# Every third V row of block 3 and every second of the sample goes to TensorE in the layer 1 mixer of a two-layer encoder

## The chip, the cores and the metric

The kernel runs on one core of a Trainium2 chip, as one program. The metric is its device time in microseconds (us). TensorE (PE) multiplies matrices into PSUM, VectorE (DVE), ScalarE (ACT) and GpSimd (POOL) work on tiles in SBUF, SyncE (SP) only issues transfers, and 16 DMA engines carry all of these.

## What is computed

Two layers, each a mixer and then PEER, a mixture of 16384 one-row experts. There are 512 prompt tokens (four blocks b0 to b3 of 128) and 64 sample tokens (s). Of the reference this matters here:

```python
# peer_u, peer_v: (2, 16384, 1024) float32; 8 heads, 16 experts for each head and token
x = x + jnp.concatenate([o_da, o_ml, o_cm], axis=-1) @ w_out   # end of the mixer
xn2 = rmsnorm(x, norm2_g)
x = x + peer(xn2, peer_wq, peer_keys, peer_u, peer_v)
...
# peer, for a block xi: e (t, 8, 16) experts by top-k of q @ keys, g their softmax
act = gelu(einsum('thkd,td->thk', u_tab[e], xi))
return einsum('thk,thkd->td', (g * act), v_tab[e])             # sum over 128 rows of v_tab
```

So each token needs 128 rows of `peer_u`, and then the sum of 128 rows of `peer_v`, each times one number.

## The kernel before

**Two ways to do PEER.** Two blocks of a layer are dense (b0 and b1 in layer 0, b2 and b3 in layer 1): in `peer_dense` every expert is computed, 128 at a time (a chunk): 8 matmuls of `U` into `H` (L1059), gelu on ACT (L1068), the gate product on DVE (L1092), and 4 matmuls of `V` into `y` (L1099). The other tokens are gathered. For each of a block's 128 expert slots `gather` (L960) has POOL fetch one row for each of the 128 partitions, 512 KB in all, into one of six `row` buffers. `gather_u` multiplies it with `xn` on DVE and sums along the row (L984); `gather_v` does

`x = row * hb[:, k] + x`

on DVE (L996), where column k of `hb` holds the gate times the activation of slot k. The sample has 64 such slots, since its two halves of experts lie on two halves of the partitions; at its end L1001 and L1002 add the lower half to the upper through a transfer (`up`).

**The order.** The stages of a layer stand in `ORDER`: for layer 1 norm (N1), projections (P1, Q1), attention and recurrence (M1), output projection (O1), expert scores (S1) of b0, b1 and s, then the same for b2 and b3 (N2 to O2), with the choice of experts of the first group (F1) among them. A scheduler lays out each engine's instructions in advance, from priorities and modelled times; the engines then run these orders, waiting on semaphores. Gathered rows have a low priority (`low`) and fill gaps. b3's V rows of layer 0 are left for layer 1: stage R, woven into M1, calls `rest_v`, which emits four rows at a time, each tied behind the last DVE instruction emitted by then. In the trace they run from 1776 to about 2040 us, the sample's U rows of layer 1 from about 2080, its V rows from 2231 to 2355, and the rows of b0 and b1 from 2510 to 3546, beside the dense blocks.

**PSUM** has eight banks of 128x512 f32. In the mixer they are `mm` (4, projections, attention, recurrence), `tr` (3, transposes) and `o` (1), by `PS_BUFS`. `LAG` says how many chunks `H` runs ahead of `y` in `peer_dense`.

**Norms.** A norm's reciprocal root (`rstd`, L226 to L231) is a chain of eleven tiny DVE instructions. In attention it ends in L608 and L609 (`on`), which PE waits for to transpose (L214) and to project (L396). The norm before the scores scales by a diagonal that ACT makes (L204, `dr`), and PE multiplies with it (L216).

Of the kernel before, what the change touches and what calls it, by code (L numbers as in the profile page):

```python
# [9 lines left out]
F32 = mybir.dt.float32  # L10
# [5 lines left out]
AF = mybir.ActivationFunctionType  # L16
ALU = mybir.AluOpType
AX = mybir.AxisListType
PSUM = bass.MemoryType.PSUM
DRAM = bass.MemoryType.DRAM  # L20

P = 128
# [21 lines left out]
MID = 10 ** 6  # L44
LOW = 10 ** 7
PS_TAG = {"p": "mm", "a": "mm", "r": "mm", "o": "o", "tp": "tr", "ta": "tr", "tr": "tr"}
PS_BUFS = {"mm": 4, "tr": 3, "o": 1}
T_TAG = {"p": "t", "a": "t", "r": "tr"}
T_BUFS = {"t": 4, "tr": 2}
DENSE_T = 4  # L50
LAG = [4, 8]
PRE = [1, 2]
EARLY_LEADS = 5
REST_STEP, REST_PARTS = 4, 16
# [38 lines left out]
def weave(*streams):  # L93
    live = [[g, n, 0] for g, n in streams]
    while live:
        r = min(live, key=lambda r: r[2] / r[1])
        r[2] += 1
        try:
            next(r[0])
        except StopIteration:  # L100
            live.remove(r)


def run(gen):
    for _ in gen:
        pass
# [14 lines left out]
class Build:  # L121
# [16 lines left out]
    def mixer_pools(self, ec, l):  # L138
        tc = self.tc

        def pool(name, bufs, **k):
            return ec(tc.tile_pool(name=name, bufs=bufs, reuse_waits="tile", **k))
        self.kvp = pool("kv", 1)
        self.mx = pool("mix", 1)
        self.t2 = pool("tmp", 1)
        self.xg = pool("xg", 1)
        self.wp = pool("wts", 3)
        self.whp = None if l else self.gp
        self.pm = pool("pmm", 1, space=PSUM)
        self.mixer = True  # L150

    def dense_pools(self, ec, l):
        tc = self.tc
# [24 lines left out]

    def psum(self, shape, st="p"):
        tag = PS_TAG[st] if self.mixer else "mm"  # L180
        ps = self.pm.tile([P] + list(shape), F32, tag=tag, name="ps", bufs=PS_BUFS[tag] if self.mixer else 3)
        return ps

    def ptile(self, st="p"):
# [804 lines left out]
        if t.sample:  # L989
            nc.vector.memset(x[NS:P], 0.0)  # L990

    def gather_v(self, t, k0, k1, tie=None):
        nc, n, x = self.nc, t.n, self.x[t.name]
        for k in range(k0, min(k1, t.npair)):
            row = self.gather(t, "peer_v", k)
            op = nc.vector.scalar_tensor_tensor(x, row, t.hb[:, k:k + 1], x, op0=ALU.mult, op1=ALU.add)  # L996
            if tie is not None:
                self.behind(op, tie)
        if t.sample and k1 >= t.npair:
            up = self.ca.tile([P, DM], F32, tag="xn", name="up", bufs=1)  # L1000
            nc.sync.dma_start(up[:NS], x[NS:P])  # L1001
            nc.vector.tensor_tensor(x[:n], x[:n], up[:n], op=ALU.add)  # L1002
# [6 lines left out]

    def rest_v(self, t, step):  # L1010
        for k in range(0, t.npair, step):
            self.low(self.gather_v, t, k, min(k + step, t.npair), self.last_dve())
            yield

    def gate_batch(self, blocks, i0, t0, pb):
# [32 lines left out]
    def peer_dense(self, l, group, xT):  # L1048
        nc, h, lag = self.nc, self.h, LAG[l]
        ys = [self.py.tile([P, 2, 512], F32, tag=f"y{i}", name=f"y{i}") for i in range(len(group))]  # L1050
# [66 lines left out]
    def run(self):  # L1117
        tc = self.tc
        self.S = Tok("s", NS, None)
        self.B = [Tok(f"b{i}", P, i) for i in range(4)]  # L1120
        self.setup()
        S, B = self.S, self.B
        g1, g2 = [B[0], B[1], S], [B[2], B[3]]
        for t in [S] + B:
            t.npair = 64 if t.sample else P
            t.c0 = TD if t.sample else (t.blk % 2) * P
        for l in range(DEPTH):
            D = g2 if l else g1[:2]
            for i, t in enumerate([S] + B):
                t.dense, t.order, t.early = t in D, i, t.sample  # L1130
            self.sel = self.ca.tile([P, TD // 8, 4, 8], F16, tag="sel", name="sel")
            self.select_pool()
            with ExitStack() as es:
                self.mixer_pools(es.enter_context, l)
                L = self.layer_params(l)
                steps = {
                    "N1": lambda: [(self.norm_in(l, L, g1), 1)], "N2": lambda: [(self.norm_in(l, L, g2), 1)],
                    "P1": lambda: [(self.project_a(l, L, g1), 4)], "Q1": lambda: [(self.project_b(l, L, g1), 2)],
                    "P2": lambda: [(self.project_a(l, L, g2), 4)], "Q2": lambda: [(self.project_b(l, L, g2), 2)],
                    "M1": lambda: self.mix(l, L, g1), "M2": lambda: self.mix(l, L, g2),  # L1140
                    "O1": lambda: [(self.out_proj(l, g1), 2)], "O2": lambda: [(self.out_proj(l, g2), 2)],
                    "S1": lambda: [(self.scores(l, L, g1), 18)], "S2": lambda: [(self.scores(l, L, g2), 18)], "F1": lambda: [(self.finish_select(l, g1), 3)],
                    "R": lambda: [(self.rest_v(B[3], REST_STEP), REST_PARTS)]}
                for part in ORDER[l].split():
                    weave(*[s for k in part.split("+") for s in steps[k]()])
                if l == 0:
                    self.low(lambda: run(self.finish_select(l, g2)), by=MID)
            with ExitStack() as es:
                self.dense_pools(es.enter_context, l)
                nlead = LAG[l] + 8 * PRE[l]  # L1150
                if l == 0:
                    xT = self.split(self.dx.tile([P, KC, TD], F32, tag="xTd", name="xTd"))
                    self.norm_T(D, Q_G2, L, xT)
                    dense = self.peer_dense(l, D, xT)
                    weave((self.first_gate(l), 32), (itertools.islice(dense, nlead), nlead))
                else:
                    sc = self.scores(l, L, g2)
                    next(sc)
                    dense = self.peer_dense(l, D, self.xT2)
                    weave((itertools.islice(dense, EARLY_LEADS), EARLY_LEADS), (sc, 18))  # L1160
                    run(itertools.islice(dense, nlead - EARLY_LEADS))
                    run(self.finish_select(l, g2))
                    self.gated = self.last_dve()
                    self.close_scores(es.enter_context, l)
                    run(self.first_gate(l))
                run(dense)
            for t in [S] + B:
                if not t.dense:
                    self.low(self.gather_u, l, L, t, None if l and t.sample else self.gated)
                    if l or t is not B[3]:  # L1170
                        self.low(self.gather_v, t, 0, P)
        self.fg = self.lp.tile([P, R_N], F32, tag="row", name="fg")[:, :DM]
        self.nc.sync.dma_start(self.fg, self.bcast_rows(self.h["final_g"], DM))
        for t in [S] + B:
            self.final(t)
# [91 lines left out]
```

## Time and profile before

| | us |
|---|---|
| time, median of 3 runs | 3598.27 |
| lowest and highest run | 3591.49, 3602.72 |
| profiled run: time | 3593.99 |
| its span, first to last instruction | 3592.2 |
| PE, DVE, ACT busy in the span | 3078.9, 2568.6, 669.8 |
| layer 0 (mixer, dense) | 0 to 640, 640 to 1640 |
| layer 1 mixer | 1640 to 2510 |
| layer 1 choice of experts, gates; dense to the end | 2510 to 2680; 2680 to 3592 |

1.79 us of the profiled run lie around its span. Busy time of an engine is the time in which at least one of its instructions runs, so a share near 1 in a stage means that the engine has no gap there, not that it works at its peak. The granted clock is that of TensorE as a share of 2.4 GHz, as a mean over the stretch (its two levels are 1.2 and 2.4 GHz).

### The profile page before, as it was taken

The numbers are of one execution on the slowest core, as the hardware profiler recorded it, in microseconds if no ns is written. First come the engines' busy times: TensorE is split into PE (matmuls) and PEld (weight loads), VectorE is DVE, ScalarE is ACT, GpSimd is POOL, SyncE is SP. The second block draws the span as 40 slices with busy tenths as digits, with TensorE's granted clock in tenths as the row PEclk, the third lists the DMA queues.
The fourth block names the chain that finished last, engine by engine and source line by source line (L and its number), as shares of the span: only waits on it lengthen the run. The fifth ranks groups of instructions, "written<-read, shape, count | busy, mean of one in ns | idle before, by whom it ended". The sixth has DMA issues, their size and how long they took to land.

```text
span 3592.2 us, 41429 instructions
## 1 busy us (share of the span) xinstructions
PE 3078.9 (86%) x13384; PEld 2057.7 (57%) x13384; DVE 2568.6 (72%) x5915; ACT 669.8 (19%) x2589; POOL 1540.9 (43%) x1284
## 2 busy tenths in 40 slices
PE   8989877789999999996977896589636999999996
PEld 6767646646666666653543654267512666666663
DVE  4454777776787666667688898847997679666664
ACT  4444222400121000001221222122210012000000
POOL 0000000065545445547657335610777666565562
PEclk9999989889999999998978997699858999999998
DMA  5332322289999999999979687853989999999995
GB/s 182 101 98 82 95 91 86 80 327 409 386 341 392 409 407 398 409 409 376 352 225 349 237 317 276 287 192 114 339 290 380 409 386 358 404 397 393 407 400 214
DMA packets 299929, 1060.21 MB, mean 295 GB/s; under 512 B 36372, under 2 KB 39232, under 8 KB 299712
## 3 DMA queue, kind: packets, MB, share of 16 engines
q0 software_dynamic: 184320, 671.17, 49.7%
q1 hardware_dynamic: 115392, 386.38, 29.9%
q8 instruction: 107, 1.75, 0.2%
q14 instruction: 110, 0.90, 0.1%
HBM read 1048.09 MB, written 8.27 MB: 294 GB/s over the span
## 4 chain that ended last, share of the span: by engine, by line
PE 44%; DVE 17%; DMA 16%; issue 14%; POOL 7%; ACT 2%; SPq 0%; POOLq 0%; DVEq 0%; ACTq 0%
PE H L1059 12%; PE y L1099 11%; DMA row<-in_peer_v_dram,idx 10%; PE ps L396 7%; POOL row L960 7%; PE ps L407 6%; DVE row L984 4%; DMA row<-in_peer_u_dram,idx 3%; DVE x_b L996 2%; PE ps L216 1%; PE ps L1028 1%; PE ps L572 1%; PE ps L830 1%; PE ps L574 1%; DVE o L1020 1%
## 5 line engine op out<-in xcount | busy, mean ns | idle before, releaser
L960 POOL DMA_INDIRECT row<-in_peer_u_dram,idx x640 | 776.6, 1213 | 1456.4 <-DVE row L984 822.4
L960 POOL DMA_INDIRECT row<-in_peer_v_dram,idx x640 | 764.1, 1194 | 542.4 <-DVE x_b L996 277.6
L984 DVE SCALAR_TENSOR_TENSOR row<-row,xn 128x1024 f32<-128x1024 f32 x640 | 769.8, 1221 | 178.1 <-DMA row<-in_peer_u_dram,idx 169.0
L1099 PE MATMUL y<-V,A 128*128 128x512 f32 x1856 | 845.4, 604 | 32.2 <-DMA V<-in_peer_v_dram 32.0
L996 DVE SCALAR_TENSOR_TENSOR x_b<-row,hb,x_b 128x1024 f32<-128x1024 f32 x512 | 656.2, 1282 | 158.5 <-DMA row<-in_peer_v_dram,idx 150.0
L1099 PEld LDWEIGHTS y<-V,A 128*128 128x128 f32 x1856 | 356.2, 194 | 421.5 <-issue 398.5
L1059 PE MATMUL H<-xT,U 128*128 128x256 f32 x2048 | 475.3, 385 | 35.2 <-ACT A L1068 20.4
L1059 PE MATMUL H<-xTd,U 128*128 128x256 f32 x2048 | 468.5, 382 | 10.2 <-ACT A L1068 8.2
L1059 PEld LDWEIGHTS H<-xT,U 128*128 128x128 f32 x2048 | 384.5, 191 | 125.8 <-ACT A L1068 39.4
L1059 PEld LDWEIGHTS H<-xTd,U 128*128 128x128 f32 x2048 | 386.7, 191 | 103.9 <-issue 40.4
L407 PE MATMUL ps<-xT,w 128*128 128x320 f32 (+1 forms) x1280 | 336.4, 417 | 28.3 <-DMA w<-in_wt_dram 17.2
L1068 ACT ACTIVATE A<-H 128x256 f32<-128x256 f32 x232 | 88.9, 383 | 1346.2 <-PE H L1059 751.2
L407 PEld LDWEIGHTS ps<-xT,w 128*128 128x128 f32 x1280 | 244.3, 195 | 95.4 <-issue 13.3
L1092 DVE TENSOR_TENSOR A<-A,W 128x256 f32<-128x256 f32 x232 | 96.8, 422 | 217.5 <-ACT A L1068 209.6
L1030 ACT ACTIVATE W<-ps 128x64 f32<-128x64 f32 x1024 | 137.8, 321 | 295.7 <-PE ps L1028 202.7
L1028 PE MATMUL ps<-o,o 128*128 128x64 f16 x2048 | 85.9, 199 | 119.6 <-DVE o L1024 119.6
L996 DVE SCALAR_TENSOR_TENSOR x_s<-row,hb,x_s 128x1024 f32<-128x1024 f32 x128 | 164.1, 1282 | 32.9 <-DMA row<-in_peer_v_dram,idx 31.1
L1028 PEld LDWEIGHTS <-o 128*128 128x128 f16 x2048 | 79.9, 102 | 151.5 <-DVE o L1024 75.4
L1099 PE MATMUL y<-V,pre 128*128 128x512 f32 x192 | 105.0, 704 | 38.9 <-DMA V<-in_peer_v_dram 31.1
L396 PE MATMUL ps<-w,xT 128*128 128x512 f32 (+3 forms) x320 | 128.9, 554 | 5.7 <-DMA w<-in_wn_dram 5.7
L351 DVE TENSOR_TENSOR wl<-w,wh 128x1024 fp32r<-128x1024 f32 (+1 forms) x56 | 64.4, 1150 | 75.9 <-PE ps L396 56.0
L396 PE MATMUL ps<-w,mix 128*128 128x512 f32 (+1 forms) x224 | 110.9, 648 | 5.8 <-DMA w<-in_wn_dram 4.2
(314 smaller groups left out, 3004.6 us busy)
## 6 DMA issues: line engine op xcount, KB each, us to landing
V<-in_peer_v_dram SPq DMA_DIRECT2D x256, 512.0 KB
U<-in_uT_dram SPq DMA_DIRECT2D x256, 512.0 KB
w<-in_wt_dram SPq DMA_DIRECT2D x96, 512.0 KB
w<-in_wn_dram SPq DMA_DIRECT2D x80, 512.0 KB
row<-in_peer_u_dram,idx POOLq DMA_INDIRECT x640
row<-in_peer_v_dram,idx POOLq DMA_INDIRECT x640
w<-in_keysT_dram SPq DMA_DIRECT2D x16, 256.0 KB
w<-in_wn_dram SPq DMA_DIRECT2D x8, 264.0 KB
```

The source lines that it names most:

```text
L351: self.nc.vector.tensor_tensor(lo, src, hi.bitcast(F32), op=ALU.subtract)
L396: self.nc.tensor.matmul(p[:t.n, :wd], x[kk][:, t.c0:t.c0 + t.n], ww[:, k * wd:(k + 1) * wd], start=(kk + part + j == 0), stop=(kk == KC - ...
L407: self.nc.tensor.matmul(ps, ww[:, k * P:(k + 1) * P], x[k][:, :n], start=(k + part + j == 0), stop=(k == KC - 1 and part == pair and j == ...
L960: self.nc.gpsimd.indirect_dma_start(out=row, out_offset=None, in_=self.h[tab], in_offset=bass.IndirectOffsetOnAxis(ap=t.idx[:, k:k + 1], a ...
L984: nc.vector.scalar_tensor_tensor(row, row, 1.0, xn, op0=ALU.mult, op1=ALU.mult, accum_out=hb[:, k:k + 1])
L996: op = nc.vector.scalar_tensor_tensor(x, row, t.hb[:, k:k + 1], x, op0=ALU.mult, op1=ALU.add)
L1028: nc.tensor.matmul(pb[:, j, :nq], o2[:, j // 2, :, j % 2], o1[:, p, j // 2, :, j % 2], start=(p == 0), stop=(p == 1))
L1030: nc.scalar.activation(W[:, :, t0:t0 + 8].rearrange("p i t -> p t i"), pb[:, :, 8 * i:8 * i + 8], AF.Copy, scale=1.0 / GSCALE)
L1059: mm = nc.tensor.matmul(hp, U[:, k, :], xT[k], start=(k == 0), stop=(k == KC - 1))
L1068: nc.scalar.activation(a, hp, AF.Gelu)
L1092: gated = nc.vector.tensor_tensor(a, a, Ws[ci // 8][:, ci % 8, :], op=ALU.mult)
L1099: nc.tensor.matmul(ys[i][:, hf, :], a[:, i * P:(i + 1) * P], V[:, hf * 512:(hf + 1) * 512], start=(c == 0), stop=(c == NCH - 1))
```

## The change

- In `gather_v` with `pe` set, each `pe`-th row doesn't go to DVE. ACT makes the diagonal matrix `dk` from the identity and column k of `hb`, and two matmuls of 128x512 in f32 add `dk` times the row to `acc`, two PSUM banks. After the last row one DVE instruction adds `acc` to `x`.
- This is set for b3 in layer 1's stage R (every third row, 42 of 128) and for the sample in layer 1 (every second, 32 of 64).
- The two banks come from the mixer's of layer 1: `mm` has 3 and `tr` 2 there.
- The sample's rows of layer 1 are emitted at the end of the mixer, not behind the dense part.
- `LAG` of layer 0 goes from 4 to 3.

```diff
-PS_BUFS = {"mm": 4, "tr": 3, "o": 1}
+PS_BUFS = [{"mm": 4, "tr": 3, "o": 1}, {"mm": 3, "tr": 2, "o": 1}]
+ON_PE = {"s": 2, "b3": 3}
-LAG = [4, 8]
+LAG = [3, 8]
...
+        self.acc = pool("vacc", 1, space=PSUM) if l else None
...
-    def gather_v(self, t, k0, k1, tie=None):
+    def gather_v(self, t, k0, k1, tie=None, pe=0):
         nc, n, x = self.nc, t.n, self.x[t.name]
         for k in range(k0, min(k1, t.npair)):
             row = self.gather(t, "peer_v", k)
+            if pe and k % pe == pe - 1:
+                if k == pe - 1:
+                    t.acc = self.acc.tile([P, 2, 512], F32, tag="acc", name="acc")
+                dk = self.sm.tile([P, P], F32, tag="dk", name="dk", bufs=2)
+                nc.scalar.activation(dk, self.ident, AF.Copy, scale=t.hb[:, k:k + 1])
+                for hf in range(2):
+                    nc.tensor.matmul(t.acc[:, hf], dk, row[:, hf * 512:(hf + 1) * 512], start=(k == pe - 1), stop=(k + pe >= t.npair))
+                continue
             op = nc.vector.scalar_tensor_tensor(x, row, t.hb[:, k:k + 1], x, op0=ALU.mult, op1=ALU.add)
             if tie is not None:
                 self.behind(op, tie)
+        if pe and k1 >= t.npair:
+            nc.vector.tensor_tensor(x, t.acc.rearrange("p a b -> p (a b)"), x, op=ALU.add)
...
-            self.low(self.gather_v, t, k, min(k + step, t.npair), self.last_dve())
+            self.low(self.gather_v, t, k, min(k + step, t.npair), self.last_dve(), ON_PE["b3"])
...
+                else:
+                    self.low(self.gather_u, l, L, S)
+                    self.low(self.gather_v, S, 0, P, None, ON_PE["s"])
...
-                if not t.dense:
-                    self.low(self.gather_u, l, L, t, None if l and t.sample else self.gated)
+                if not t.dense and not (l and t.sample):
+                    self.low(self.gather_u, l, L, t, self.gated)
```

Lines behind the edit have other numbers in the changed kernel (L996 becomes L1007, L609 L611, L396 L398); its rows of `dk` are L1002, of `acc` L1005, and the closing addition is L1011.

On DVE in stage M2, layer 1, the end of the chain for the first block's `on`, before (L229 to L231 with 4 columns, L608 and L609 are the chain, L996 the sample's V rows):

```order
L996 SCALAR_TENSOR_TENSOR x_s<-row,hb,x_s 128x1024
L230 SCALAR_TENSOR_TENSOR rs_t<-rs_t,rs_v 128x4
L230 SCALAR_TENSOR_TENSOR rs_t<-rs_t,rs_v 128x8
L996 SCALAR_TENSOR_TENSOR x_s<-row,hb,x_s 128x1024
L231 SCALAR_TENSOR_TENSOR rs_y<-rs_t,rs_y 128x4
L231 SCALAR_TENSOR_TENSOR rs_y<-rs_t,rs_y 128x8
L996 SCALAR_TENSOR_TENSOR x_s<-row,hb,x_s 128x1024
L608 TENSOR_TENSOR rs_y<-rs_y,rz 128x4
L229 TENSOR_TENSOR rs_t<-rs_y 128x8
L996 SCALAR_TENSOR_TENSOR x_s<-row,hb,x_s 128x1024
L609 TENSOR_TENSOR on<-ps,rs_y 128x512
```

And in the changed kernel at the same place:

```order
L231 TENSOR_TENSOR rs_t<-rs_y 128x4
L1007 SCALAR_TENSOR_TENSOR x_s<-row,hb,x_s 128x1024
L578 TENSOR_REDUCE z<-ps 128x1
L737 SCALAR_TENSOR_TENSOR dn<-nd 128x8
L232 SCALAR_TENSOR_TENSOR rs_t<-rs_t,rs_v 128x4
L738 TENSOR_TENSOR dn<-dn,ex 128x8
L233 SCALAR_TENSOR_TENSOR rs_y<-rs_t,rs_y 128x4
L739 RECIPROCAL dn<-dn 128x8
L610 TENSOR_TENSOR rs_y<-rs_y,rz 128x4
L740 TENSOR_TENSOR nd<-nd,dn 128x8x64
L611 TENSOR_TENSOR on<-ps,rs_y 128x512
```

Of the eleven instructions shown four are rows before, and one is now. From the chain's first L226 to `on`, rows of either token on DVE number before and now: in M1 12 and 5 (s), 12 and 6 (b0), 4 and 0 (b1); in M2 12 and 3 (b2), 4 and 0 (b3).

On PE, where O1 begins in layer 1, the changed kernel has this (`mix` is the mixer's output; L754 and the like stand just ahead). Before, the L396 rows of `w` and `mix` stand there without any other:

```order
L1005 MATMUL acc<-row,dk 128x512 x4
L398 MATMUL ps<-w,mix 128x512 x4
L398 MATMUL ps<-w,mix 64x512 x2
L398 MATMUL ps<-w,mix 128x512 x4
L398 MATMUL ps<-w,mix 64x512 x2
L1005 MATMUL acc<-row,dk 128x512 x4
L398 MATMUL ps<-w,mix 128x512 x7
```

Each x4 of `acc` is two rows of b3. In PE's order 24 of the 42 come before this place, eight in O1, two in the norm behind it and eight in S1; of the sample's 32, 18 come before O2's first projection and 14 in O2. On DVE 19 of b3's rows are left behind that norm.

In the dense part of layer 1 PE's order changes too. Before, two chunks alternate:

```order
L1059 MATMUL H<-xT_14654,U 128x256 x16
L1099 MATMUL y_14714<-V,A 128x512 x2
L1099 MATMUL y_14715<-V,A 128x512 x2
L1099 MATMUL y_14714<-V,A 128x512 x2
L1099 MATMUL y_14715<-V,A 128x512 x2
L1059 MATMUL H<-xT_14654,U 128x256 x16
```

In the changed kernel single chunks do, and SP loads `V` and `U` in turn instead of two and two:

```order
L1072 MATMUL H<-xT_15296,U 128x256 x8
L1112 MATMUL y_15356<-V,A 128x512 x2
L1112 MATMUL y_15357<-V,A 128x512 x2
L1072 MATMUL H<-xT_15296,U 128x256 x8
L1112 MATMUL y_15356<-V,A 128x512 x2
L1112 MATMUL y_15357<-V,A 128x512 x2
```

The order of layer 0's dense part was this already; there `LAG` only takes one `H` away from the start.

## Rows read from the trace of the kernel before

**Rows 1.** The page: busy time, share of the span and instructions of each engine.
```profile
PE 3078.9 (86%) x13384; PEld 2057.7 (57%) x13384; DVE 2568.6 (72%) x5915; ACT 669.8 (19%) x2589; POOL 1540.9 (43%) x1284
```

**Rows 2.** Windows by stage: length, busy time and instructions of engines, clock, DMA.
```profile
core 0: us, PE busy (x) PEld busy (x) DVE busy (x) ACT busy (x) POOL busy (x), PEclk, DMA share, GB/s
...
1776.00:1906.00 130.00, 90.19 (x397) 57.93 (x396) 111.06 (x218) 33.88 (x147) 74.36 (x60) 0.75 0.80 255
1906.00:1947.00 41.00, 41.00 (x86) 14.10 (x85) 32.49 (x31) 0.19 (x1) 29.54 (x24) 0.93 0.97 369
1947.00:1966.00 19.00, 10.63 (x54) 8.29 (x52) 18.44 (x37) 11.23 (x33) 13.64 (x10) 0.73 0.93 323
1966.00:2085.00 119.00, 104.17 (x485) 77.08 (x485) 108.21 (x435) 30.55 (x122) 47.52 (x44) 0.94 0.75 269
2085.00:2196.00 111.00, 79.58 (x263) 49.11 (x261) 104.86 (x385) 16.51 (x34) 45.55 (x43) 0.89 0.85 317
2196.00:2296.00 100.00, 71.04 (x257) 44.45 (x258) 81.42 (x157) 26.40 (x83) 54.55 (x45) 0.70 0.80 245
2296.00:2359.00 63.00, 38.30 (x97) 18.57 (x96) 47.09 (x56) 6.02 (x19) 38.31 (x34) 0.77 0.93 342
```

**Rows 3.** Waits of PE, 1776 to 1966 us: total, times, longest.
```profile
PE ps L214 <- DVE on L609: 25.4, 3, 12.2
PE ps L216 <- ACT dr L204: 8.4, 1, 8.4
```

**Rows 4.** Waits of PE, 2196 to 2369 us.
```profile
PE ps L214 <- DVE on L609: 36.4, 2, 21.8
PE ps L507 <- DVE cc L503: 24.4, 1, 24.4
```

**Rows 5.** Timeline of PE, 2255 to 2290 us: two neighbouring rows.
```profile
2259.86 0.70 PE L574 MATMUL ps<-bias,cst 128*128 128x256 f32 x2
2282.35 1.12 PE L214 MATMUL ps<-cst,on 128*128 128x128 f32 x4 [21.79 <-DVE on L609]
```

**Rows 6.** Windows, the V rows on DVE (L996) alone: length, busy time and count, clock, DMA.
```profile
1776.00:1906.00 130.00, 77.59 (x61) 0.75 0.80 255
1906.00:1947.00 41.00, 28.81 (x24) 0.93 0.97 369
...
1966.00:2085.00 119.00, 41.51 (x33) 0.94 0.75 269
```

**Rows 7.** The chain that ended last: start, us, what (O1, sample's rows, kernel's end).
```profile
1906.64 39.41 PE ps L396 x80
...
2231.30 1.27 DVE x_s L996
...
2353.69 1.30 DVE x_s L996
2355.00 7.97 DMA up<-x_s
...
3545.11 1.30 DVE x_b L996
...
3565.47 3.67 PE y L1099 x8
```

**Rows 8.** Windows in the dense parts of layer 0 and 1, columns as in rows 2.
```profile
1187.00:1587.00 400.00, 390.92 (x1345) 256.86 (x1345) 268.43 (x337) 25.62 (x63) 197.49 (x196) 0.99 1.02 406
3100.00:3500.00 400.00, 387.21 (x1320) 248.35 (x1319) 260.17 (x363) 23.84 (x62) 238.16 (x194) 1.00 1.02 400
```

**Rows 9.** The page: the V rows on DVE, b3's and the sample's among them.
```profile
L996 DVE SCALAR_TENSOR_TENSOR x_b<-row,hb,x_b 128x1024 f32<-128x1024 f32 x512 | 656.2, 1282 | 158.5 <-DMA row<-in_peer_v_dram,idx 150.0
L996 DVE SCALAR_TENSOR_TENSOR x_s<-row,hb,x_s 128x1024 f32<-128x1024 f32 x128 | 164.1, 1282 | 32.9 <-DMA row<-in_peer_v_dram,idx 31.1
```

**Rows 10.** O1's projections on PE, 1906 to 1966 us: ns of one, least, median, most.
```profile
L396 PE MATMUL ps<-w,mix x88: 592/592/1220, 1906.6 to 1949.0; 128*128 128x512 f32 x56, 128*64 128x512 f32 x32
```

**Rows 11.** ACT's diagonals, 1640 to 2400 us.
```profile
L204 ACT ACTIVATE dr<-cst,rs_y x10: 345/386/402, 1655.3 to 2369.0; 128x128 f32<-128x128 f32 x8, 64x64 f32<-64x64 f32 x2
```

**Rows 12.** Waits of DVE for V rows, 1776 to 2040 and 2196 to 2369 us.
```profile
DVE x_b L996 <- DMA row<-in_peer_v_dram,idx: 15.0, 16, 2.7
DVE x_s L996 <- DMA row<-in_peer_v_dram,idx: 16.9, 14, 3.5
```

**Rows 13.** Waits of PE, 3100 to 3500 us.
```profile
PE H L1059 <- ACT A L1068: 12.8, 27, 0.5
```

More of the change, by code (lines that the diff above doesn't have):

```diff
@@ L148, in mixer_pools @@
         self.whp = None if l else self.gp
+        self.acc = pool("vacc", 1, space=PSUM) if l else None
         self.pm = pool("pmm", 1, space=PSUM)
-        self.mixer = True
+        self.mixer = l + 1
     def dense_pools(self, ec, l):
@@ L180, in psum @@
         tag = PS_TAG[st] if self.mixer else "mm"
-        ps = self.pm.tile([P] + list(shape), F32, tag=tag, name="ps", bufs=PS_BUFS[tag] if self.mixer else 3)
+        ps = self.pm.tile([P] + list(shape), F32, tag=tag, name="ps", bufs=PS_BUFS[self.mixer - 1][tag] if self.mixer else 3)
         return ps
```

## The prediction

> **What bounds the kernel now.** The page says that no engine is full: PE is busy for 86% of the span and DVE for 72% [rows 1]. That average says little of the stages that the change touches, so the stages come next [rows 2]. The reader is to compare PE and DVE with the length of each. In M1 with b3's rows (1776 to 1906) neither is full: DVE 111 of 130 us, PE 90, at a granted clock of 0.75. In O1 PE has no gap, 41.0 of 41. In S1 and behind it, up to 2196, DVE carries 108.2 + 104.9 = 213 of 230 us and PE 184. M2 and O2 (2196 to 2359) are again full on neither: PE 109, DVE 128 of 163, at clocks of 0.70 and 0.77.
>
> Why stages with idle engines last so long is seen in PE's waits. In M1 it waited three times, 25.4 us in all, for `on`, and then 8.4 us for a diagonal that ends another norm [rows 3]. In M2 it waited 36.4 us for `on` in two waits [rows 4]. The timeline shows the longest: behind a small matmul at 2259.86 nothing runs on PE until 2282.35 [rows 5]. `on` ends a chain of tiny DVE instructions, and the order put a V row between nearly all of them: 12 rows in that chain. V rows took 77.6 us of DVE in M1, 28.8 in O1 and 41.5 in S1 [rows 6]. The chain that ended last runs through PE in O1 (39.41 us for 80 matmuls), through the sample's V rows from 2231.30 to 2355.00, then `up`, which nothing hides, and at the end through the last V row of b1 at 3545 and what stands behind it [rows 7]. The dense part that leads there is full of transfers: the DMA share is 1.02, at 400 GB/s, in layer 1, and 1.02, at 406, in layer 0 [rows 8].
>
> **The change part by part.** A V row costs DVE 1.282 us [rows 9]. 42 and 32 rows leave it: 53.8 and 41.0 us of DVE time, less two closing additions that I put at 1.3 us each, as that row's shape. The same row on PE is two matmuls of 128x512 in f32, and each is two records: 4 records. At the kernel's end 8 such records took 3.67 us on the chain, 0.459 each [rows 7], so a row costs 4 x 0.459 = 1.84 us. In O1 it is 39.41 / 80 x 4 = 1.97. A slow record lasted 1.22 us against 0.592 [rows 10], so at the lower clock a row may cost up to twice, 3.7 us. I take 1.84; 74 rows are 136 us of PE, for 92 us of DVE. What counts is where they stand.
>
> *M1.* 24 PE rows add 44 us to PE's 90.2: 134 in a stage of 130. Were the clock as in O1, 0.93, the 90.2 would be about 90.2 x 0.75 / 0.93 = 73, and the sum 117. DVE falls: 61 rows become 43 by the end of M1. In the three chains to `on` 17 rows fewer stand, 17 x 1.28 = 22 us of the 25.4 that PE waited. So the stage passes from DVE's chains to PE's sum. I take -5 us; bounds -13 (117) and +10 (134, and waits of PE for its rows).
>
> *O1.* Eight rows in a stage in which PE has no gap: 8 x 1.84 = +14.7. Fetching doesn't hold it up: 24 gathers went out in these 41 us, 1.71 us each [rows 2], and eight PE rows need 24. I take +14; bounds +12 (a slightly better clock) and +20 (each PE row waiting 0.7 us).
>
> *The norm behind O1.* Two PE rows fall into the 8.4 us in which PE waited anyway; fewer V rows stand in the norm's chain. -2; bounds -6 and +2.
>
> *S1 to the start of M2.* DVE is the bound here. Of b3's rows 33 were left for S1 [rows 6], now 19: 18 us less on DVE, and 1.3 more for the addition. PE gets 8 x 1.84 = 15 and stands at 199 of 230. PE's scores feed DVE's choice of experts, so not all comes through: -13; bounds -17 and 0.
>
> Together b3's part gives -5 + 14 - 2 - 13 = -6 us; its bounds add up to -24 and +32.
>
> *M2 and O2.* Here 32 of 64 rows go to PE: 59 us on top of 109.3, 168 in 163 us at the clock it had; at 0.93 the 109.3 become about 86, and the sum 145. The 12 rows in the longest chain become 3. The sample's 64 V rows took 2231.3 to 2355.0, 1.93 us each [rows 7]; at O1's 1.71 they would take 109, 14 us less. The end (`up` 7.97 us, its addition) stays, and the addition of `acc` comes ahead of it, +1.3. The 24.4 us that PE waited for `cc` just before [rows 4] are DVE's own U rows and stay. I take -9; bounds -13 and +6 (168 - 163, and the addition).
>
> *The dense part of layer 1.* Chunks alternate singly now, as in layer 0. PE waited 12.8 us in 400 for ACT's read of `H` when two `H` came in a row [rows 13]: 23 us in the 720 from 2780 to 3500 if all of that counted. But transfers are at their limit in both layers, and there the single order moved 406 GB/s against 400 [rows 8]: 1.5% of 720 = 11 us. I take half, -6; bounds 0 and -11.
>
> *The rest.* 74 diagonals on ACT cost 0.386 us each [rows 11], 29 us on an engine that is busy for 33.9 of 130 us in M1 and 0.19 in O1 [rows 2]: nothing, with a wait of one diagonal (0.4 us) for each of the 22 rows in O1 and O2 as the other bound, 9 us if none is made ahead. No row shows what one bank less of `mm` and `tr` costs. A tile in O1 is 16 matmuls, 7.9 us, and its read by DVE is far shorter, so there it is covered; in M1 and M2 tiles are small. 0, upper bound 8, as the wait for `dr` [rows 3]. `LAG` 3 in layer 0: 0, bounds -3 and +3, since that part is full of transfers.
>
> The sum is -6 - 9 - 6 = -21 us on the profiled 3593.99, so 3573. The median of the runs lies 4.28 above that run, so the forecast is 3598.27 - 21 = 3577 us.
>
> A rule of the Trainium skill speaks against the change: by TensorE: Matmul & The Clock Gate (engine queue depth), PE takes only weight loads ahead of matmuls under way, so a matmul that waits for its row holds up all behind it. The trace agrees for such a wait: nothing ran on PE in the 21.79 us [rows 5]. It is part of the slower rival.
>
> **The rivals.** *PE becomes the bound (slower).* If the clock stays near 0.75 and 0.70, M1 needs 134 and M2 with O2 168 us: +4 and +5, with O1's +14.7. PE's rows then stand in order among its matmuls, and each may wait for its transfer as DVE did: 16 and 14 waits took 15.0 and 16.9 us, 1.06 each [rows 12]; 22 rows in O1 and O2 make 23 us. Less the 13 of S1 and the 6 of the dense part: 4 + 5 + 15 + 23 - 19 = +28, about 3626 us. It decides when PE's busy share in M1 and M2 comes to 0.95. For it speaks that both sums already reach the stage's length; against it that the low clock stands where PE has gaps.
>
> *Nothing comes of it.* M1 and M2 go by the transfers, not by DVE: their DMA share is already 0.80, and M2's rows can't come sooner than their fetches. Then M1 and M2 give 0, O1 costs 14, S1 returns 13, and the dense part gives nothing: about 3598. For it: a share of 0.93 in O2 [rows 2].
>
> *The clock rises with PE's work (larger gain).* All lower bounds together: -24 - 13 - 11 = -48, about 3550 us. For it: in O1, where PE has no gap, 0.93 was granted; in M1, with 40 us of gaps, 0.75. The Trainium skill has this as a rule (TensorE: Matmul & The Clock Gate, part 1): the clock is low by default and activity lifts it. The trace agrees between stages; that added rows do it within M1, no row shows.
>
> **How the numbers follow.** This kernel's runs lie within 0.3%, 11 us, so less than that can't be told from no change. The forecast (a gain of 8 to 35 us) has 0.44, the larger gain 0.19, nothing 0.19, PE as the bound 0.18. Faster by over 0.3% are the larger gain and all but 0.02 of the forecast: 0.61. Within it lie nothing and that rest: 0.21. Slower: 0.18. The range runs from the larger gain, 3547, to the weaker half of the slower case, 3608. The likeliest case alone is 3563 to 3590.
>
> **What would show it.** Right: PE's waits for `on` in M1 and M2 fall from 25.4 and 36.4 to under 15 each; the clock of M1 and M2 rises over 0.85; O1 lasts 53 to 58 us with a gapless PE; the stretch from its end to M2 is some 15 us shorter; M2's start lies some 6 us earlier and the sample's last row some 15; single chunks in the dense part take 7.1 us. Wrong: waits of PE for `row` or `dk` of more than 20 us in all, waits for a bank (PE behind a read of `ps`), a gap between the sample's rows as long as before, or a dense part that is longer than before although it begins earlier.

## The result, and the profile after

The changed kernel takes 3647.40 us (median of 3 runs, 3644.64 to 3660.74) against 3598.27: 1.0153 times as long, 95% interval 1.0119 to 1.0186. It is slower by 49 us; 3577 was forecast. Beside the kernel before on another chip it was 1.0155 (1.0124 to 1.0185). The profiled run took 3647.4 us, its span 3645.6.

The page, in the columns of [rows 1]:

```profile
PE 3194.5 (88%) x13680; PEld 2095.5 (57%) x13680; DVE 2487.8 (68%) x5843; ACT 700.3 (19%) x2663; POOL 1545.4 (42%) x1284
```

DVE lost 81 us and PE gained 116, where 92 and 136 had been costed. Where the time went is seen by cutting both programs at the same instructions. Both columns come from traces of one chip (the runs `before_again` and `change_again` below):

| from, to | before, us | changed, us | difference |
|---|---|---|---|
| start, first transposes of layer 1 (L216) | 1656.1 | 1663.0 | +6.9 |
| there, the first transposes of the norm before S2 (the mixer) | 707.0 | 725.5 | +18.5 |
| there, V matmuls of layer 1's 17th chunk | 403.8 | 404.4 | +0.6 |
| 17th to 97th chunk | 587.9 | 615.4 | +27.5 |
| there, end | 228.5 | 226.8 | -1.7 |

The sum, +52, is the difference of the spans (3635.0 - 3583.4 = 51.6). Over half of it lies in the dense part, where no row was moved. The other cut points of the first two traces give +7, +26 and +27.5.

**The dense part.** The timeline of the changed kernel on PE, then on ACT (start, length, what, idle time before it and what ended it):

```profile
3300.45 3.72 PE L1072 MATMUL H<-xT,U 128*128 128x256 f32 x16 [0.47 <-ACT A L1081]
3304.01 3.60 PE L1112 MATMUL y<-V,A 128*128 128x512 f32 x8
3308.07 3.72 PE L1072 MATMUL H<-xT,U 128*128 128x256 f32 x16 [0.47 <-ACT A L1081]
...
3300.01 0.39 ACT L1081 ACTIVATE A<-H 128x256 f32<-128x256 f32 x1 [7.24 <-PE y L1112]
3307.64 0.38 ACT L1081 ACTIVATE A<-H 128x256 f32<-128x256 f32 x1 [7.24 <-PE y L1112]
```

A chunk takes 3308.07 - 3300.45 = 7.62 us. The gelu doesn't start when its `H` is done (3304.0) but when the V matmuls behind it are (3307.64), and the next `H` waits for the gelu. So the three stand in a row: 3.56 + 3.60 + 0.47. Before, one `H` in two waited [rows 13]. Windows and PE's wait in the same stretch as [rows 8]:

```profile
3100.00:3500.00 400.00, 374.88 (x1258) 234.31 (x1257) 246.57 (x369) 23.35 (x61) 231.97 (x183) 1.00 1.00 381
...
PE H L1072 <- ACT A L1081: 25.1, 53, 0.5
```

The transfers fell from 400 to 381 GB/s and the gathers from 194 to 183: they follow here, they don't set the pace.

**The mixer.** Windows by stage: Q1, M1, O1, the norm, S1, the rest to M2, M2, O2, each between the landmarks of this trace; columns as in [rows 2].

```profile
1769.00:1801.00 32.00, 30.60 (x106) 19.39 (x105) 15.76 (x32) 5.42 (x16) 20.59 (x15) 1.00 0.91 336
1801.00:1898.00 97.00, 89.93 (x407) 51.32 (x406) 64.86 (x141) 31.85 (x124) 54.61 (x46) 0.98 0.80 248
1922.00:1970.00 48.00, 47.07 (x108) 17.16 (x106) 28.64 (x27) 3.19 (x7) 26.88 (x24) 1.00 0.86 303
1970.00:1991.00 21.00, 14.81 (x43) 8.66 (x44) 13.52 (x33) 10.40 (x29) 12.16 (x12) 0.76 0.91 308
1991.00:2120.00 129.00, 121.32 (x553) 85.77 (x553) 102.22 (x467) 35.41 (x135) 47.21 (x39) 1.00 0.65 233
2120.00:2221.00 101.00, 77.25 (x252) 47.59 (x251) 96.99 (x340) 17.43 (x36) 44.99 (x39) 0.90 0.87 332
2221.00:2330.00 109.00, 98.52 (x329) 55.27 (x327) 67.77 (x143) 33.78 (x101) 54.18 (x49) 0.82 0.79 242
2330.00:2397.00 67.00, 58.96 (x151) 27.17 (x150) 24.32 (x36) 10.67 (x29) 29.47 (x29) 0.92 0.84 299
```

PE has taken DVE's place: it is busy for 0.93 of M1 and 0.90 of M2. Before, it was busy for 71.2 of M1's 97 us from 1786 on, 0.73, and for 0.71 of M2 [rows 2]. The granted clock rose with it, in M1 from 0.75 to 0.98. PE's waits in M1 to the norm, then in M2 and O2 (answering [rows 3, 4]), and POOL's in M1 to the norm:

```profile
PE acc L1005 <- DMA row<-in_peer_v_dram,idx: 8.5, 6, 4.3
PE ps L216 <- DVE rs_t L232: 3.6, 1, 3.6
PE ps L216 <- DVE on L611: 1.3, 1, 1.3
...
PE acc L1005 <- DMA row<-in_peer_v_dram,idx: 13.8, 4, 6.7
...
POOL row L962 <- PE acc L1005: 34.0, 11, 9.0
```

The waits for `on` are nearly gone, as forecast. Of 25.4 us 1.3 are left, and 3.6 that the profile puts down to an earlier instruction of such a chain (L232); of the 36.4 in M2 none is left.

What the stages gained or lost can't be read from these windows: in the changed order 16 of the 88 records of O1's projections stand ahead of 1922. So both programs are cut at the same instructions once more: M1's first matmul, the first of the 88 records, and S1's first projection, three rows from before and three from the changed kernel:

```profile
1785.62 3.97 PE L507 MATMUL ps<-cc,mlw 128*128 128x320 f32 x8 [2.25 <-DVE cc L503]
1906.57 43.05 PE L396 MATMUL ps<-w,mix 128*128 128x512 f32 x88
1966.01 4.30 PE L407 MATMUL ps<-xT,w 128*128 128x320 f32 x15
...
1800.65 0.70 PE L509 MATMUL ps<-cc,mlw 128*128 128x320 f32 x2
1916.33 8.35 PE L398 MATMUL ps<-w,mix 128*128 128x512 f32 x16
1994.02 1.34 PE L409 MATMUL ps<-xT,w 128*128 128x320 f32 x4
```

M1 so cut takes 121.0 us before and 115.7 now, O1 with the norm 59.4 and 77.7. The same cuts in other traces (the runs follow below): the order of before in `before`, `before_again`, `before_tie` and `before_lag3`; all 74 rows on PE in the changed kernel's two traces and `dense_tie`; half of their matmuls in `half_acc`.

| stretch, us | forecast | order of before | all rows on PE | half the matmuls |
|---|---|---|---|---|
| from the first L216 to M1 (Q1 at its end) | none | 127.8 to 130.8 | 132.2 to 137.9 | 132.7 |
| M1 | -5 | 118.5 to 121.0 | 111.3 to 115.9 | 116.6 |
| O1 and the norm | +12 | 58.3 to 59.8 | 76.2 to 77.7 | 64.7 |
| S1 to M2 | -13 | 225.2 to 230.2 | 225.8 to 229.3 | 227.1 |
| M2 and O2 | -9 | 153.6 to 162.6 | 166.1 to 176.8 | 137.0 |

So M1 became a little shorter, O1 with the norm and M2 with O2 longer, and S1 to M2 stayed. The timeline of PE in Q1 shows what I had not counted there:

```profile
1776.23 1.98 PE L1005 MATMUL acc<-row,dk 128*128 128x512 f32 x4 [1.40 <-DMA row<-in_peer_v_dram,idx]
1778.05 4.47 PE L409 MATMUL ps<-xT,w 128*128 128x320 f32 x16
1782.36 1.88 PE L1005 MATMUL acc<-row,dk 128*128 128x512 f32 x4
1784.07 4.47 PE L409 MATMUL ps<-xT,w 128*128 128x320 f32 x16
```

Four rows stand among projections that leave no gap, 1.72 us of PE's order each (1784.07 - 1782.36 = 1.71).

### The profile page after: what moved, and what is told of

It reads as the page before. It is cut to its first block, busy times and chain, and to the rows that moved or that the text cites. A ratio compares the mean times of both kernels' runs of the same rounds, so it can differ in the third digit from the quotient of the medians.

```text
span 3645.6 us, 42022 instructions
## 1 busy us (share of the span) xinstructions
PE 3194.5 (88%) x13680; PEld 2095.5 (57%) x13680; DVE 2487.8 (68%) x5843; ACT 700.3 (19%) x2663; POOL 1545.4 (42%) x1284
## 4 chain that ended last, share of the span: by engine, by line
PE 43%; issue 17%; DMA 15%; DVE 12%; POOL 10%; ACT 2%; SPq 0%; POOLq 0%; DVEq 0%; ACTq 0%
PE H L1072 12%; PE y L1112 10%; POOL row L962 10%; DMA row<-in_peer_v_dram,idx 10%; PE ps L409 7%; PE ps L398 5%; DMA row<-in_peer_u_dram,idx 4%; DVE row L986 3%; PE acc L1005 2%; PE ps L832 1%; PE ps L574 1%; DVE x_b L1007 1%; PE ps L1041 1%; PE ps L576 1%; DMA w<-in_wt_dram 1%
## 5 line engine op out<-in xcount | busy, mean ns | idle before, releaser
L962 POOL DMA_INDIRECT row<-in_peer_u_dram,idx x640 | 786.7, 1229 | 1468.9 <-DVE row L986 812.1
L1007 DVE SCALAR_TENSOR_TENSOR x_b<-row,hb,x_b 128x1024 f32<-128x1024 f32 x470 | 603.1, 1283 | 156.7 <-DMA row<-in_peer_v_dram,idx 149.7
L1005 PE MATMUL acc<-row,dk 128*128 128x512 f32 x296 | 151.8, 647 | 25.0 <-DMA row<-in_peer_v_dram,idx 25.0
L1007 DVE SCALAR_TENSOR_TENSOR x_s<-row,hb,x_s 128x1024 f32<-128x1024 f32 x96 | 123.1, 1283 | 51.4 <-DMA row<-in_peer_v_dram,idx 49.8
L398 PE MATMUL ps<-w,xT 128*128 128x512 f32 (+3 forms) x320 | 134.6, 572 | 19.6 <-DVE gt L462 7.8
L914 DVE MAX8 v<-s 128x8 f32<-128x128 f32 x128 | 32.9, 283 | 124.9 <-ACT s L835 124.8
```

The lines of the kernel that those rows point to most:

```text
L398: self.nc.tensor.matmul(p[:t.n, :wd], x[kk][:, t.c0:t.c0 + t.n], ww[:, k * wd:(k + 1) * wd], start=(kk + part + j == 0), stop=(kk == KC - ...
L962: self.nc.gpsimd.indirect_dma_start(out=row, out_offset=None, in_=self.h[tab], in_offset=bass.IndirectOffsetOnAxis(ap=t.idx[:, k:k + 1], a ...
L1005: nc.tensor.matmul(t.acc[:, hf], dk, row[:, hf * 512:(hf + 1) * 512], start=(k == pe - 1), stop=(k + pe >= t.npair))
```

## The experiments

Theory A, on the dense part: the scheduler let `H` run one chunk further ahead, eleven in place of ten, while `A` has ten buffers (`LAG` + 2). Then each gelu waits for the V matmuls that read its buffer, and these stand directly behind its `H`. Theory B: transfers or gathered rows set that pace. Theory C, on the mixer: a row on PE costs its 1.8 us wherever PE has no gap (Q1, O1, the norm, S1, O2), and nothing in M1 and M2. Rival D: what costs is that PE waits in order for rows and holds their buffers, in M1 and M2 above all.

Times are medians beside the kernel before on the same chip, whose median there was 3584.81 to 3589.26. The first four expectations go by the first chip's 3598 and 3647; the chip that ran them gave 11 us less. "Mixer" is the stretch of the table above. Four traces with the order of before in the mixer gave 713, 707, 704 and 696 us, so less than some 10 us of it says nothing by itself.

**The dense order alone.** In the changed kernel, and in the kernel before:

```diff
+                if k == 0 and l and 0 <= c - lag - 2 < len(ym):
+                    self.behind(mm, ym[c - lag - 2].ins)
...
+                ym.append(mm)
```

`mm` is the first matmul of a chunk's `H`, `ym` holds the last V matmul of each chunk.

> The changed kernel, with the first matmul of each H of layer 1's dense part ordered behind the V matmuls ten chunks back, so that H runs ten chunks ahead and not eleven. Theory A (with eleven ahead and ten A buffers, the gelu of a chunk waits for the V matmuls just behind its H, and the next H for that gelu): the period falls from 7.63 us per chunk to 6.9 to 7.15, PE's wait for the gelu vanishes, and the time comes to 3590 to 3615. Theory B (the transfers, or DVE's gathered rows, set the period and the wait only shows it): the period stays above 7.5 and the time within 10 us of 3647.

> The kernel before, with the same tie alone: single chunks, ten ahead, in place of pairs. Theory A: 7.26 us per chunk falls to 6.9 to 7.15, the time to 3575 to 3592. Theory B: within 8 us of 3598.

`dense_tie`: 3608.48 us, 1.0060 (1.0038 to 1.0082), so 0.9 of the 1.5 per cent is gone. Its timeline on PE, and PE's waits from 3100 to 3500:

```profile
3300.15 3.62 PE L1072 MATMUL H<-xT,U 128*128 128x256 f32 x16
3303.61 3.60 PE L1114 MATMUL y<-V,A 128*128 128x512 f32 x8
3307.04 3.62 PE L1072 MATMUL H<-xT,U 128*128 128x256 f32 x16
...
PE H L1072 <- DMA U<-in_uT_dram: 2.4, 1, 2.4
PE y L1114 <- DMA V<-in_peer_v_dram: 0.5, 1, 0.5
```

6.89 us a chunk, and no wait for the gelu: theory A. The 80 chunks take 584.1 us in place of 615.4. That is less of a gain than 0.73 a chunk, since in the 24 chunks around the matmuls for further gates (2972 to 3087 us) a chunk takes 7.96 us with the tie and 7.84 without. `before_tie`: 3581.43 us, 0.9980 (0.9956 to 1.0003), 583.2 us for the 80 chunks against 587.9. Its time fits both theories, since the kernel before took 3586.85 there; its steady chunk, 6.89 us with no wait for the gelu, fits A alone. Pairs lose little, since one `H` in two waits; what ten ahead gives is small.

In the kernel before, with the other order brought about by layer 0's `LAG` alone:

```diff
-LAG = [4, 8]
+LAG = [3, 8]
```

> The kernel before with LAG of layer 0 at 3 and nothing else; its order of layer 1's dense part becomes single chunks, eleven ahead, as in the changed kernel. Theory A: 7.63 us per chunk there (+20 to +27) and +3 to +6 in layer 0: 22 to 33 us over the kernel before. Rival (that dense order costs only together with the moved rows): within 8 us of it.

3612.32 us, 1.0079 (1.0051 to 1.0107), 28 us over the kernel before. Its timeline on PE, and its wait:

```profile
3302.58 3.72 PE L1059 MATMUL H<-xT,U 128*128 128x256 f32 x16 [0.47 <-ACT A L1068]
3306.13 3.60 PE L1099 MATMUL y<-V,A 128*128 128x512 f32 x8
3310.20 3.72 PE L1059 MATMUL H<-xT,U 128*128 128x256 f32 x16 [0.47 <-ACT A L1068]
...
PE H L1059 <- ACT A L1068: 24.6, 52, 0.5
```

The same 7.62 us and the same 615.4 us for 80 chunks, without one V row moved. A number of layer 0 set off the order of layer 1. `LAG` 3 with the changes of the mixer left out in part (`sample_only`, `b3_only`) gave pairs again, so it isn't `LAG` as such. What makes the scheduler choose between the two orders no run shows.

**One token at a time.** `ON_PE` with one entry at 0:

```diff
-ON_PE = {"s": 2, "b3": 3}
+ON_PE = {"s": 2, "b3": 0}
...
+ON_PE = {"s": 0, "b3": 3}
```

> The changed kernel with all of b3's rows back on DVE; the sample's half stays on PE. Its dense order is that of pairs again, as before. Theory A (dense order +27, the projections and M1 to S1 +19, M2 and O2 about +9, layer 0 +6): 3647 - 27 - 19 = about 3601. Rival (the sample's rows are what costs in the mixer): above 3612.

> The changed kernel with all of the sample's rows back on DVE; b3's third stays on PE. Dense order in pairs. Theory A: 3647 - 27 - 9 = about 3611. Rival (the sample's rows are what costs): below 3603.

`sample_only`: 3587.26, 1.0000 (0.9977 to 1.0023), mixer 703. `b3_only`: 3603.13, 1.0044 (1.0021 to 1.0068), mixer 723. Both have pairs in the dense part, and with the chip's 11 us taken off both lie within 4 us of theory A's forecast (3590 and 3600). So b3's rows make the mixer's loss; the sample's make none that can be told. `sample_only` has the fewer PSUM banks too: rows and banks together cost nothing that can be told there.

**PE's time, or the waiting?** Half of the matmuls, with ten ahead:

```diff
-                for hf in range(2):
+                for hf in range(2 if k == pe - 1 else 1):
...
```

> The changed kernel with ten chunks ahead in the dense part, and one matmul of the two for each PE row but the first of each token: the second half of the columns of those rows is left out of the sum. It takes 66 us of PE out, some 33 of it from Q1, O1, O2, the norm and S1. Theory C (what the rows cost is PE's own time in stages that PE fills): 15 to 33 us less than with both matmuls, so from 12 us under the kernel before to 6 us over it. Rival D (PE waits in order for the rows and holds their buffers): at least 14 us over the kernel before.

3573.76 us, 0.9971 (0.9951 to 0.9991), 11 us under the kernel before where both matmuls gave 21 over it. Its order isn't quite the same (22 of b3's rows stand ahead of O1 and after Q1 in place of 20, 17 of the sample's in O2 in place of 14). PE still waits 19.0 us for rows, against 23.9 in `dense_tie`. By the two ratios that is 32 us less, the upper edge of what theory C allowed. The mixer is 684 us against 729 in `dense_tie`, of which M2 and O2 make 137 against 173, though only some 29 us of PE left these two. So with all 32 rows PE's time was the bound there, and rows in M2 weren't quite free, as theory C had it. M1 is no shorter for it (116.6 us against 111.3), so PE's time doesn't bound M1.

**Which rows?** 17 of b3's on PE, in M1 alone; these and 18 of the sample's, in M2 alone; the other 25 of b3; the 14 of the sample in O2. All with ten ahead. The lines are those of `m1_m2_rows`. In the others the slots differ, `ON_PE` is 0 for a token without rows on PE, and `b3_other_rows` has `not 12 <= k < 63` as its condition:

```diff
+PE_K = {"s": (0, 36), "b3": (12, 63)}
...
-            if pe and k % pe == pe - 1:
...
+            lo, hi = PE_K.get(t.name, (0, 0))
+            if pe and k % pe == pe - 1 and lo <= k < hi:
...
```

> Only 17 of b3's rows on PE, those that fall into M1 (slots 12 to 62); none in Q1, O1, the norm or S1, and none of the sample's. Ten chunks ahead in the dense part. Theory C: M1 costs nothing, so the time is that of the kernel before with the same dense order, 0 to 10 us under the kernel before. Rival D: M1 is longer for it, at least 8 us over the kernel before.

> The same, and 18 of the sample's rows on PE, those that fall into M2 (slots 0 to 35), none in O2. Theory C: 5 to 20 us under the kernel before, since M2's long wait for the attention's norm goes and O2 is left alone. Rival D: M2 is as long as with all 32 rows, 109 us against 101, and the time at least 5 us over the kernel before.

> The counterpart of the run with M1's rows: on PE stand only b3's 25 rows outside M1 (slots below 12 and from 63), in Q1, O1, the norm and S1; none of the sample's. Ten chunks ahead in the dense part. Theory C: these make the loss: 25 x 1.84 = 46 us of PE, of which 10 to 25 arrive at the end, so 5 to 20 us over the kernel before. Rival D (M1's rows, which hold the row buffers until PE comes to them, make it): within 6 us of the kernel before or under it.

> On PE stand only the sample's 14 rows from slot 37 on, which fall into O2; b3 is all on DVE. Ten chunks ahead in the dense part. Theory C: O2 grows by up to 14 x 1.84 = 26 us, and 5 to 18 of it arrive at the end: the kernel before and up to 13 us over it, against 7 us under it for that dense order alone. Rival D: under the kernel before by as much as the dense order gives, since no row in M2 waits.

| | time, us | ratio, interval | mixer, us |
|---|---|---|---|
| `before_tie` | 3581.43 | 0.9980 (0.9956 to 1.0003) | 696 |
| `b3_m1_rows` | 3580.70 | 0.9984 (0.9961 to 1.0008) | 708 |
| `m1_m2_rows` | 3571.16 | 0.9960 (0.9941 to 0.9979) | 694 |
| `b3_other_rows` | 3619.45 | 1.0103 (1.0047 to 1.0160) | 728 |
| `o2_rows` | 3579.48 | 0.9981 (0.9965 to 0.9997) | 696 |

b3's rows outside M1 make the whole loss, 23 us of mixer over the 705 that the four traces average; those in M1 make none. That is theory C, and what rival D said of M1's rows falls. The time of `b3_other_rows`, 30 us over the kernel before, is more than the 5 to 20 that theory C allowed; its trace came to layer 1 12 us later than the changed kernel's (1674.9 against 1662.8), behind a part in which no row was moved. What D means does occur in it: of PE's 17.8 us of waits for rows 12.2 are one wait, just ahead of O1.

For the sample theory C was wrong about O2: 14 rows there changed neither the time nor the mixer. [Rows 2] had the reason: in O2 PE was busy for 38.3 of 63 us before, so 14 x 1.84 = 26 us could go into 25 us of gaps, where O1 had none. D's forecast for that run came true, but D falls with `m1_m2_rows`, which is 14 us under the kernel before where D asked for 5 over it. `m1_m2_rows` and `o2_rows` are the versions of the change that are faster than the kernel before, by 0.2 to 0.6% and by up to 0.35%. Both intervals overlap with that of `before_tie`, which moves no row, so no gain of the moved rows is shown.

Windows of M1 in `b3_m1_rows`, `half_acc` and `b3_other_rows`, and PE's longest wait for a bank in the last, from 1780 to 2230 us:

```profile
1789.00:1885.00 96.00, 86.64 (x393) 50.77 (x394) 66.42 (x142) 30.52 (x121) 49.87 (x45) 0.95 0.79 243
...
1803.00:1902.00 99.00, 89.86 (x373) 52.44 (x372) 68.17 (x145) 31.62 (x121) 57.11 (x49) 0.84 0.82 261
...
1809.00:1905.00 96.00, 73.25 (x333) 47.10 (x332) 76.78 (x154) 24.10 (x99) 47.88 (x40) 0.76 0.70 216
...
PE ps L398 <- DVE gt L462: 13.7, 1, 13.7
```

By such windows M1 lasts 93 to 101 us in all traces, with 331 matmul records or 411, with DVE at 65 us or 81. Up to O1's projections it is 114.9 and 115.0 us in the two runs that have b3's rows on PE in M1 alone, against 118.5 to 121.0 with none, so the chains to `on` gave some 5 us and no more. What holds M1 there no run shows. The last line is a wait for a bank, with `mm` at 3. In the first trace of the changed kernel two such waits of `L398`, behind the reads at L450 and L462, took 11.5 us in the projections between S1 and M2, and 4.1 before; but the wait for `cc` behind them [rows 4] fell from 24.4 to 8.9, so they stand in place of a wait that was there anyway.

**The same two kernels on one chip.**

> The changed kernel once more, beside the others on one chip: about 1.015 times the kernel before. With ten chunks ahead it was 1.006, so 0.009 of it, some 30 us, is the dense order by theory A.

> The kernel before, for a trace from the same chip. Stages within 3 us of the first trace except M2 with O2, which other runs with the same order there showed at 153 us and not 163.

`change_again`: 3641.10 us, 1.0155 (1.0124 to 1.0185). `before_again`: 3585.22 us, one run. The timelines have the cut points of the table, the first two rows from `before_again`, the others from `change_again`:

```profile
1656.14 4.64 PE L216 MATMUL ps<-dr,x_b 128*128 128x128 f32 x24 [21.73 <-ACT dr L204]
2363.10 3.14 PE L216 MATMUL ps<-dr,x_b 128*128 128x128 f32 x13 [8.74 <-ACT dr L204]
...
1662.99 3.78 PE L218 MATMUL ps<-dr,x_b 128*128 128x128 f32 x16 [20.39 <-ACT dr L206]
2388.46 2.93 PE L218 MATMUL ps<-dr,x_b 128*128 128x128 f32 x12 [6.52 <-ACT dr L206]
```

M2 with O2 took 161 us in `before_again`, against 163, 161 and 154 in the other three traces of that order: the 10 us that were expected of the chip are the spread of single runs.

## Why the prediction was wrong

**The dense part** is the step that failed first. I read "single chunks, as in layer 0" and took layer 0's rate: -6 us, bounds 0 and -11. Measured: +27.5 in the changed kernel, and `before_lag3` gives the same by itself. The pattern of `H` and `y` was layer 0's, its offset was not. In layer 0's steady part four or five `H` stood ahead, below the `LAG` + 2 buffers of `A`; in the changed layer 1 eleven, for ten. This could be counted before any run: `H` less `y` ahead of a V matmul in PE's order, against the buffers. The row that priced it was there too: 0.47 us for each `H` that waits [rows 13], but I used it only as a gain to be had. (A chunk with the wait is in all 0.73 us longer, 7.62 against 6.89.) A dense part that is longer than before stood among the signs of being wrong, but neither a rival nor a term of the sum held it, so the slower side of the range stood on the mixer alone.

That `H` waits for a gelu that reads the other half of the tile agrees with a rule of the Trainium skill (PSUM — Partial Sum Buffer, PSUM bank collisions raise a hardware error): PE may not write a bank while another engine reads it, whatever the address, so accesses are to be guarded by bank. Both halves of `H` are one bank here. No run put them into two.

**M1**, -5 forecast, -5.6 measured between the averages of the two groups of traces, and some -5 in the two runs with M1's rows alone. The number was right, the reason was not. The waits for `on` fell and the clock rose from 0.75 to 0.98, as the rival with the larger gain had it, and its 13 us didn't come. But PE's sum, which I took for the new bound, wasn't it either: with half of the matmuls M1 lasted 116.6 us. I placed 24 rows here; 17 were run in M1 itself, three behind it, and four in Q1 (7.6 us of PE by the windows of `acc`). There PE was busy for 25.2 of 29 us before, so they didn't fit: the stretch up to M1 grew by some 5 us, which the sum didn't have. I looked only at stages from 1776 on.

**O1 and the norm**, +14 and -2: measured +18. Ten rows stand there, and 10 x 1.84 is 18.4: each cost its full price. I had let the norm's two vanish in its wait.

**S1 to M2**, -13 forecast, next to nothing measured (226 to 229 us against 225 to 230). The term that was mis-sized is DVE's relief. DVE was busy for 199 us in place of 213, but it waited more: for the scores, behind PE, and for rows. Its waits before (1966 to 2196), then in the changed kernel (1991 to 2221):

```profile
DVE x_b L996 <- DMA row<-in_peer_v_dram,idx: 3.2, 4, 2.0
DVE v L912 <- ACT s L833: 1.5, 1, 1.5
...
DVE x_b L1007 <- DMA row<-in_peer_v_dram,idx: 14.5, 11, 4.0
DVE v L914 <- ACT s L835: 11.6, 4, 5.7
```

The wait for the scores `s` is 9.9 to 12.9 us in each of the six traces with b3's rows on PE in S1, and at most 1.5 in the others. PE came to 121 of the 129 us from 1991. The sum kept back 5 of DVE's 18 us for what waits on PE; nearly all of them went. The sample's gathers, which need those scores, began 96 us into this stretch, at 2090, and 92 before (at 2058, not at about 2080).

**M2 and O2**, -9 forecast, some +12 measured; in `sample_only`, with the same rows, it was 167 us, and the mixer as a whole no longer than before. PE was busy for 157 us, near the 168 that I computed for an unchanged clock, though the clock rose to 0.86. `half_acc` shows that this PE time was the bound: I had let the gain from DVE's chains outweigh it.

**`LAG`**, 0 with bounds of 3: +5.6 at the end of layer 0's dense part in this trace (1642.6 against 1637.0), +3.2 in `before_lag3`. But `before_tie`, with `LAG` at 4, ended it at 1641.5, so most of this is the spread of single runs.

The rival in which PE becomes the bound was priced at +28 for 3626 us and had 0.18. For the mixer it came true, at +18 to +26. Its mechanism was right where PE had no gap, and wrong in that waits for rows would make half of the price: PE waited 25 us for rows in all, and `half_acc` kept 19 of them and lost the cost.

What stays open is why the scheduler's choice in the dense part flips with such distant numbers, and what holds M1.

## What to carry to other kernels

Work that is moved to another engine costs its full time wherever that engine has no gap, so a stage's two busy shares are compared before and after, stage by stage, from the first stage that the new order reaches. Where the other engine waits for results of the one that gets the work, its relief can be lost in that wait. Two orders are compared between the same instructions; windows set by eye can put one stage's work into the next. In a ring of buffers count how far the producer runs ahead in the new order: one step more than there are buffers put producer, reader and consumer in a row here, and over 80 turns that cost more than the whole change was meant to save. Where a scheduler lays out the program, a change in one place is tested with the order of the others held.

## What the runs showed of the hardware

The granted clock took back much of PE's work. In M1 PE was busy for 71 us with 331 matmul records at a clock of 0.75, for 90 with 373 at 0.84 (`half_acc`), and for 90 with 407 at 0.98: the added records were nearly free from the second step to the third. This agrees with the Trainium skill (TensorE: Matmul & The Clock Gate, part 1), by which activity lifts the clock. That added rows do it within M1, which no row of before showed, had 0.19 in the prediction; the stage was only some 5 us shorter for it.
